# Seven block products for eight in the gate and up projections of a SwiGLU layer, with one weight tile's low part made by an adding DMA

## The chip, the core and the metric

The kernel runs on one core of a Trainium2 chip. The metric is the device time of the whole program in microseconds (us), the median of several runs. PE is TensorE, which multiplies matrices; PEld is its loading of the stationary operand; DVE is VectorE, ACT is ScalarE, POOL is GpSimd, and SP issues most DMAs. Every engine works through its own queue of instructions in the order in which they stand there, and waits on semaphores for the others.

## What is computed

One decoder layer over 256 tokens of width 2048, all in float32: a mixer (attention beside a convolution, then an output projection), and a SwiGLU block, which is where the change is. Cut to that block, the reference is

```
h  = rmsnorm(x, norm_pre_ffn)                       # 256 x 2048
g  = einsum('bsd,df->bsf', h, w_gate)               # 2048 x 5632
up = einsum('bsd,df->bsf', h, w_up)                 # 2048 x 5632
f  = einsum('bsf,fd->bsd', silu(g) * up, w_down)    # 5632 x 2048
x  = x + rmsnorm(f, norm_post_ffn)
```

## The kernel before

**Products.** A float32 number is split exactly in two: a high part (its float32r rounding) and a low part (the rest). A product of activations and weights is three matmuls per k tile of 128 rows: high by high, low by high, high by low. A weight tile is 512 rows (four k tiles) by 512 columns, 1 MB. Its high part `wh` is a rounding copy on ACT (L170), its low part `wl` is the difference on DVE (L171).

**Half steps.** The program is a row of half steps, each one weight tile against one of the two blocks of 128 tokens: 8 matmuls with `wh` (pass 0, L236 and L237), then 4 with `wl` (pass 1, L239). A weight tile serves two half steps. A chunk is 512 columns of gate or up, its sum over the 16 k tiles is four weight tiles, and its two token blocks have a PSUM bank each. After the gate and the up chunk with the same number f (11 of each), ACT takes silu of gate (L753), DVE multiplies by up (L761), PE transposes the product (L768) and it is split again (L193, L194). After every four chunks (then four, then three) the down projection of these rows runs, four chunks of 512 columns, added up in SBUF (L777, L779).

**What sets the order.** It is written out by the program `run_stream`, which goes through the half steps: first side work that is due, then the split of the weight tile that takes the slot just given up, then the loading of a further tile, then the 12 matmuls. `wh` and `wl` have four slots each (NSLOT), so a tile is split when the tile four places before it has had its last matmul. Loaded weights (`w`) have three buffers (NW), and a load is issued by SP when the split that read the buffer is done.

Of the kernel before, what the change touches and what calls it, by code (L numbers as in the profile page):

```python
# [26 lines left out]
P = 128  # L27
# [28 lines left out]
def hybrid_layer_kernel(ctx: ExitStack, tc: tile.TileContext, x, xt, pack, lamv,  # L56
# [28 lines left out]
    # ------------------------------------------------------------ constants  # L85
# [50 lines left out]
    class WTile:  # L136
        """Some rows (nk tiles of 128) and 512 columns of a weight matrix."""

        def __init__(self, src, r0, nk, cols):
            self.src, self.r0, self.nk, self.cols = src, r0, nk, cols  # L140
            self.eager = False

# [32 lines left out]
    class Operand:  # L175
        """8 k tiles per part of [128, 256 tokens], as float32r h and l."""
# [20 lines left out]
    class Chunk:  # L197
        """psum[tb] = x[tb] @ one 512-column chunk."""
# [16 lines left out]
    halves = []          # (chunk, tile, k of x, token block)  # L215
    tiles = []

    def add(chunk, specs, stagger=False):
        """specs: (k of x, WTile) in order."""
        for k, t in specs:  # L220
            tiles.append(t)
        order = ([(s, tb) for tb in range(2) for s in specs] if stagger
                 else [(s, tb) for s in specs for tb in range(2)])
        for (k, t), tb in order:
            halves.append((chunk, t, k, tb))
            chunk.left[tb] += t.nk

    def one(chunk, t, k0, tb, j, pas):
        """One k tile: pass 0 is (h + l) of x with h of w, pass 1 h of x with l of w."""
# [11 lines left out]
    def matmuls(chunk, t, k0, tb):  # L241
        if t.eager:
            # k tile by k tile, both token blocks, as the first data comes in
# [12 lines left out]

    def run_stream():
        last_use, preps = {}, deque()
# [3 lines left out]
        for s, (c, t, k, tb) in enumerate(halves):  # L262
            now[0] = s
            run_side()
            while preps:
# [3 lines left out]
                if i + NW < len(tiles):  # L269
                    tiles[i + NW].dma()  # L270
# [7 lines left out]
            if c.left[tb] == 0 and c.done:  # L278
                c.done(tb)
# [13 lines left out]
    # ------------------------------------------------------------ pre norm  # L293
# [27 lines left out]
    # ------------------------------------------------------------ lambda, bias  # L321
# [3 lines left out]
    def small_setup():  # L325
# [15 lines left out]
        # -(e0 - e1 + init) = (e1 - e0) - init  # L341
# [3 lines left out]
        # r[h, m] = bias of distance m - 127, masked below  # L345
# [8 lines left out]
        # bias[q, h, k] = r[h, 255 + q - k]  # L354
# [106 lines left out]
    # ------------------------------------------------------------ attention  # L461
# [34 lines left out]
    def head(h, qT, kT):  # L496
# [13 lines left out]
        for c in range(2):  # L510
            for b in range(2):
                # e = -(scores + bias), nm = min(e)
# [13 lines left out]
        # a * sum0 = e0 - (lam sum0 / sum1) e1; 1 / sum0 follows at the output  # L526
# [17 lines left out]
    def attend(half):  # L544
# [6 lines left out]
        # aT columns: [keys 0, block 1 | keys 1, block 1 | keys 0, block 0]  # L551
# [12 lines left out]
        # columns (head, block), block 0 the later queries  # L564
# [70 lines left out]
    # ------------------------------------------------------------ mixer output  # L635
# [42 lines left out]
    rstd2 = [None, None]  # L678

# [48 lines left out]

    oc = []
# [16 lines left out]
    # ------------------------------------------------------------ SwiGLU  # L746
# [38 lines left out]
    def post_down(pi, last, n, bank):  # L785
        for tb in range(2):
            down_evac(pi, last, n, tb, bank[tb])
        if pi == 1 and n == 0:
            load_gain(1, "gpf")
# [24 lines left out]
    parts = [(0, 4), (4, 8), (8, 11)]  # L814
    for pi, (f0, f1) in enumerate(parts):
        A = Operand("act")
        last = pi == len(parts) - 1
        needs = {}
        for f in range(f0, f1):
            c = both(lambda bank, f=f: post_gate(f, bank))(Chunk("gate", H2))  # L820
            add(c, w_tiles(w_gate, 0, [(f * C, C)], 0, KT), stagger=f == 0)
            k = (f - f0) * 4

            def hook(bank, f=f, A=A, k=k):
                g = post_up(f, A, k, bank)
                j = Job(g, now[0])
# [4 lines left out]
            add(c, w_tiles(w_up, 0, [(f * C, C)], 0, KT))  # L831
            needs[k] = [lambda f=f: st_["act", f]]
        nk = (f1 - f0) * 4
        for n in range(4):
            c = Chunk("down", A, needs=needs)
            ts = w_tiles(w_down, f0 * C, [(n * C, C)], 0, nk)
            if last and n == 3:
                c.done = lambda tb, c=c, pi=pi: spawn(finish(pi, tb, c.bank[tb]))
                add(c, ts, stagger=True)
            else:  # L840
                both(lambda bank, pi=pi, last=last, n=n: post_down(pi, last, n, bank))(c)
                add(c, ts)
# [10 lines left out]
    # the first tiles come in pieces, and are split k tile by k tile  # L853
# [71 lines left out]
```

## Time and profile before

| | us |
|---|---|
| median of 3 runs (lowest, highest) | 1088.16 (1087.69, 1088.36) |
| profiled execution, first to last instruction | 1086.7 |
| PE busy in it | 1072.2 |
| DVE busy in it | 634.9 |
| ACT busy in it | 491.6 |
| gate, up and down stage, about | 370 to 1078 |

The profile is of one execution. Its span lies about 1.5 us under the median of the runs; the rest lies before the first and after the last instruction. A busy PE here means that matmuls follow each other without a gap; matmuls overlap, so the distance between two starts is the cost of one, and not its duration.

### The profile page before, as it was taken

The page shows a single profiled execution, that of the slowest core. Times are in us where ns is not written, and L with a number is a line of the kernel's source. Part 1 is how long each engine was busy: PE and PEld are TensorE (multiplying, and loading weights), DVE is VectorE, ACT ScalarE, POOL GpSimd, SP SyncE. Part 2 cuts the span into 40 slices and gives each one's busy share as a digit, 9 for nine tenths or more (in the row PEclk, how much of TensorE's full clock was granted, in tenths as well). Part 3 has the DMA queues.
Part 4 walks back from the last instruction along what each step waited for, and adds up shares of the span by engine and source line. Part 5 has one row for each costly group of instructions (what it writes and reads, how often), then busy time and mean ns, then how long its engine had stood idle before and what let it go on. Part 6 is the DMA issues. An engine that isn't in the chain of part 4 may idle for free.

```text
span 1086.7 us, 11988 instructions
## 1 busy us (share of the span) xinstructions
PE 1072.2 (99%) x4886; PEld 885.5 (81%) x4886; DVE 634.9 (58%) x733; ACT 491.6 (45%) x525; POOL 10.8 (1%) x16
## 2 busy tenths in 40 slices
PE   9999999999999999999999999999999999999996
PEld 7878788787888888888888888888888888888885
DVE  6589989898556654444544445444454444454554
ACT  6754563755645743334334334343333333333441
POOL 0000000001000000000000000000000000000000
PEclk9999999999999999999999999999999999999998
DMA  9876545444764556555555555555656555555532
GB/s 307 300 259 210 180 161 183 157 156 156 296 203 155 173 198 209 183 195 175 186 193 192 195 194 191 194 183 178 215 179 232 195 194 191 177 194 194 194 116 77
DMA packets 113686, 209.77 MB, mean 193 GB/s; under 512 B 4024, under 2 KB 23776, under 8 KB 112864
## 3 DMA queue, kind: packets, MB, share of 16 engines
q1 hardware_dynamic: 113632, 209.02, 56.9%
q8 instruction: 38, 0.62, 0.2%
q14 instruction: 16, 0.13, 0.0%
HBM read 206.89 MB, written 2.11 MB: 192 GB/s over the span
## 4 chain that ended last, share of the span: by engine, by line
PE 90%; DMA 3%; DVE 3%; ACT 2%; issue 1%; SPq 1%; POOL 1%; DVEq 0%; POOLq 0%; ACTq 0%
PE mm L236 28%; PE mm L237 28%; PE mm L239 28%; DMA w<-in_w_in_dram 3%; DVE wl L171 1%; ACT wh L170 1%; PE ft L768 1%; DVE conv_acc L397 1%; DMA rb<-in_rel_bias_dram 1%; PE scmm L236 1%; PE scmm L237 1%; PE scmm L239 1%; PE sc L505 0%; POOL hrs L97 0%; PE ht L698 0%
## 5 line engine op out<-in xcount | busy, mean ns | idle before, releaser
L171 DVE TENSOR_TENSOR wl<-w,wh 128x2048 fp32r<-128x2048 f32 (+1 forms) x200 | 432.3, 2163 | 348.6 <-ACT wh L170 345.4
L170 ACT CAST wh<-w 128x2048 fp32r<-128x2048 f32 (+1 forms) x200 | 361.2, 1808 | 345.3 <-PE mm L237 322.5
L236 PE MATMUL mm<-wh,h2h 128*128 128x512 f32 x704 | 275.2, 391 | 0.0
L237 PE MATMUL mm<-wh,h2l 128*128 128x512 f32 x704 | 274.0, 389 | 0.0
L239 PE MATMUL mm<-wl,h2h 128*128 128x512 f32 x704 | 188.3, 389 | 0.0
L239 PEld LDWEIGHTS mm<-wl,h2h 128*128 128x128 f32 x704 | 132.2, 188 | 27.6
L237 PEld LDWEIGHTS mm<-wh,h2l 128*128 128x128 f32 x704 | 132.2, 188 | 27.1
L236 PEld LDWEIGHTS mm<-wh,h2h 128*128 128x128 f32 x704 | 132.2, 188 | 27.0
L236 PE MATMUL mm<-wh,acth 128*128 128x512 f32 x352 | 137.2, 390 | 0.0
L237 PE MATMUL mm<-wh,actl 128*128 128x512 f32 x352 | 137.0, 389 | 0.0
L236 PE MATMUL mm<-wh,xh 128*128 128x512 f32 x320 | 127.4, 398 | 1.4 <-ACT wh L170 1.4
L237 PE MATMUL mm<-wh,xl 128*128 128x512 f32 x320 | 124.9, 390 | 0.0
L397 DVE SCALAR_TENSOR_TENSOR conv_acc<-conv_in,pk,conv_acc 128x255 f32<-128x255 f32 (+14 forms) x240 | 94.2, 463 | 0.0
L239 PE MATMUL mm<-wl,acth 128*128 128x512 f32 x352 | 94.1, 389 | 0.0
L239 PE MATMUL mm<-wl,xh 128*128 128x512 f32 x320 | 87.2, 390 | 0.0
L239 PEld LDWEIGHTS mm<-wl,acth 128*128 128x128 f32 x352 | 66.1, 188 | 13.8
L237 PEld LDWEIGHTS mm<-wh,actl 128*128 128x128 f32 x352 | 66.1, 188 | 13.6
L236 PEld LDWEIGHTS mm<-wh,acth 128*128 128x128 f32 x352 | 66.1, 188 | 13.6
L236 PEld LDWEIGHTS mm<-wh,xh 128*128 128x128 f32 x320 | 60.1, 188 | 15.3 <-ACT wh L170 2.4
L239 PEld LDWEIGHTS mm<-wl,xh 128*128 128x128 f32 x320 | 59.9, 188 | 13.2 <-DVE wl L171 0.6
L237 PEld LDWEIGHTS mm<-wh,xl 128*128 128x128 f32 x320 | 60.2, 188 | 11.8
L237 PE MATMUL mm<-wh,mixl 128*128 128x512 f32 x96 | 37.5, 391 | 0.3 <-DVE mixl L458 0.3
(137 smaller groups left out, 556.6 us busy)
## 6 DMA issues: line engine op xcount, KB each, us to landing
w<-in_w_gate_dram SPq DMA_DIRECT2D x44, 1024.0 KB, 5.0
w<-in_w_up_dram SPq DMA_DIRECT2D x44, 1024.0 KB, 5.0
w<-in_w_down_dram SPq DMA_DIRECT2D x44, 1024.0 KB, 5.1
w<-in_w_in_dram SPq DMA_DIRECT2D x24, 1024.0 KB, 5.0
w<-in_w_out_dram SPq DMA_DIRECT2D x16, 1024.0 KB, 5.1
w<-in_w_in_dram SPq DMA_DIRECT2D x24, 512.0 KB, 4.8
w<-in_w_in_dram SPq DMA_DIRECT2D x16, 256.0 KB, 5.8
xn<-in_x_dram SPq DMA_DIRECT2D x2, 1024.0 KB, 11.2
```

Of the source, the lines that this page charges most:

```text
L170: nc.scalar.copy(self.h[:, a:b], self.w[:, a:b])
L171: nc.vector.tensor_tensor(out=self.l[:, a:b], in0=self.w[:, a:b], in1=self.h[:, a:b].bitcast(F32), op=ALU.subtract)
L236: nc.tensor.matmul(bank, lhsT=h, rhs=t.h[:, j], start=first, stop=False)
L237: nc.tensor.matmul(bank, lhsT=l, rhs=t.h[:, j], start=False, stop=False)
L239: nc.tensor.matmul(bank, lhsT=h, rhs=t.l[:, j], start=False, stop=last)
L397: return lambda: nc.vector.scalar_tensor_tensor(out=conv_acc[:, cb, s:], in0=conv_in[:, cb, :S - s], scalar=w, in1=conv_acc[:, cb, s:], op ...
L768: nc.tensor.transpose(bk[:, j * P:(j + 1) * P], sg[:, tb, j * P:(j + 1) * P], ident)
```

## The change

It alters the gate and up chunks f = 1 to 10; chunk 0 and all of down keep their products, and down runs after three, three, three and two chunks instead of four, four and three. The lower eight k tiles of a chunk pair are computed as before: two ordinary tiles of gate (called G0 and G1 here) and two of up (U0 and U1), two half steps each. The upper eight k tiles, for both chunks and both token blocks, are a product of a 2 by 2 matrix of activation blocks and a 2 by 2 matrix of weight tiles (r11 and r21 of gate, r12 and r22 of up), and instead of eight block products it is made from seven, in the program P1 to P7, of 12 matmuls each, from sums and differences of the blocks. The class `Pair` does that:

- Sums of the activations are made once (`form_sums`), and split.
- Sums of the weight tiles are made for every pair on DVE: three in a row (`sums`, after the split of the U0 before it) and one later (`last_sum`, after the split of P3). They overwrite loaded tiles, and one of them has a `w` buffer of its own that is not loaded (x).
- Each of the seven products has a high and a low part made from its tile or sum, and one half step.
- Results are put together outside PSUM: copies of partial sums on ACT (`v`, `s`), additions on DVE (L1011, L1028, L1037).
- The four half steps of U0 and U1 of one pair are placed among the products of the next pair (`fill`), so the order is P1, U0 (2), P7, P6, U1 (2), P5, P2, G0 (2), P3, G1 (2), P4: 15 half steps, where there were 16.
- G1's low part is not a DVE difference. ACT writes the negative of the rounded tile to `wl`, and a DMA issued by POOL adds the tile, read again from DRAM, to it.
- Loads go through two queues (`pump`): three `w` buffers, and a few whole tiles (`raw`) from the general pool, to which r12, r21 and r22 go.
- To have room, the residual is written to DRAM and read back near the end.

The diff, cut to this core:

```diff
         def split(self):
             self.h = wp.tile([P, SPLIT, C], F32R, tag="wh", bufs=NSLOT, name="wh")
             self.l = wp.tile([P, SPLIT, C], F32R, tag="wl", bufs=NSLOT, name="wl")
-            self.split_part(0, self.nk)
+            if self.by_dma:
...
+                nc.scalar.activation(self.l, self.w, ACTF.Copy, scale=-1.0)
+                nc.gpsimd.dma_start(self.l, rows[:, c0:c0 + n].rearrange("(k p) c -> p k c", p=P),
+                                    accum_op=ALU.add)
+                nc.scalar.copy(self.h, self.w)
+            else:
+                self.split_part(0, self.nk)
+            free["w"] += 1
...
+    def pump(i):
+
+        for tag, q in queue.items():
+            while q and free[tag] and q[0][0] - i <= 9:
+                free[tag] -= 1
+                q.popleft()[1].load(tag)
...
                 if i < len(tiles):
                     tiles[i].split()
-                if i + NW < len(tiles):
-                    tiles[i + NW].dma()
+                    pump(i)
+                    for fn in tiles[i].post:
+                        fn()
+                    pump(i)
...
+    def form_sums():
+
+        r = v3(T("sums"), 4)
+        h, l = H2.part(1)
...
+            nc.vector.tensor_tensor(out=r[:, o], in0=r[:, a], in1=r[:, b], op=op)
+        sh, sl = v3(T("sumh", F32R), 4), v3(T("suml", F32R), 4)
+        nc.scalar.copy(sh, r)
+        nc.vector.tensor_tensor(out=sl, in0=r, in1=sh.bitcast(F32), op=ALU.subtract)
...
+        def sums(self):
+            self.sub(self.r11, self.r12, self.r11)
+            self.sub(self.r12, self.r22, self.r12)
+            self.sub(self.x, self.r22, self.r11)
+
+        def last_sum(self):
+            self.sub(self.x, self.r21, self.x)
+            free["r"] += 1
...
+            return (s[1] + fill[0] + s[7] + s[6] + fill[1] + s[5] + s[2] + g[0] + s[3] + g[1] + s[4])
...
+            elif what == 7:
+                self.b7 = ps.tile([P, 2, C], F32, tag="sc", bufs=1, name="b7")[:, 0]
...
+            if what == 1:
+                self.v = v3(M("v"), 2)
+                nc.scalar.copy(self.v[:, 0], self.b1)
+            elif what == 6:
+                nc.scalar.copy(self.v[:, 1], self.b1)
+            elif what == 5:
+                self.s = M("s")[:, :C]
+                nc.scalar.copy(self.s, self.b1)
+                nc.vector.tensor_tensor(out=self.s, in0=self.b7, in1=self.s, op=ALU.add)
+            elif what == "g1" and tb == 0:
+                self.sg = v3(M("sg"), 2)
+                self.gate(0, self.b2, self.v[:, 0])
+            elif what == 4:
+                self.gate(1, self.b7, self.v[:, 1])
+            elif what == "u1" and tb == 0:
+                self.up(0, self.b1)
+            elif what == "u1":
+                nc.vector.tensor_tensor(out=self.s, in0=self.b8, in1=self.s, op=ALU.add)
+                self.up(1, self.s)
+                st_["act", self.f] = spawn(act_put(self.A, self.k, self.sg), 2)
...
+    parts = [(0, 3), (3, 6), (6, 9), (9, 11)]
```

What the engines have in their queues is shown at three places. On DVE before, inside the chunks f = 5, from one up chunk into the next gate chunk (`wl` is a low part, `sg` the gated product, `actl` the low part of its transpose; what a row waits for stands in brackets):

```order
L171 TENSOR_TENSOR wl_4809<-w_4704,wh_4808 128x2048 [waits DMAHW3_49,PE_49,Activation_49]
L171 TENSOR_TENSOR wl_4842<-w_4752,wh_4841 128x2048 [waits DMAHW4_49,PE_49,Activation_49]
L171 TENSOR_TENSOR wl_4874<-w_4782,wh_4873 128x2048 [waits DMAHW5_49,PE_49,Activation_49]
L171 TENSOR_TENSOR wl_4904<-w_4812,wh_4903 128x2048 [waits DMAHW6_49,PE_49,Activation_49]
L171 TENSOR_TENSOR wl_4934<-w_4845,wh_4933 128x2048 [waits DMAHW7_49,PE_49,Activation_49]
L761 SCALAR_TENSOR_TENSOR sg_4838<-mm0_4847,rffn0_2921,sg_4838 128x512 [waits PE_49]
L761 SCALAR_TENSOR_TENSOR sg_4838<-mm1_4848,rffn1_3047,sg_4838 128x512 [waits PE_49]
L171 TENSOR_TENSOR wl_4966<-w_4877,wh_4965 128x2048 [waits DMAHW0_49,Activation_49]
```

Now on DVE, from the U0 of pair f = 3, through the three sums of pair 4, to that pair's P5 (rows 1 and 8 are low parts of U0 and U1, rows 2 to 4 the sums, rows 5 and 7 the gate additions of pair 3, row 6 the low part of P7, the others those of P6 and P5):

```order
L196 TENSOR_TENSOR wl_4262<-w_4200,wh_4261 128x2048 [waits DMAHW4_49,PE_49,Activation_49]
L957 TENSOR_TENSOR w_4143<-raw_4175,w_4143 128x2048 [waits DMAHW2_49,DVE_49]
L957 TENSOR_TENSOR raw_4175<-raw_4178,raw_4175 128x2048 [waits DMAHW3_49,DVE_49]
L957 TENSOR_TENSOR w_4265<-raw_4178,w_4143 128x2048 [waits DMAHW0_49]
L1011 TENSOR_TENSOR sg_4281<-b2_4202,v_4071 128x512 [waits PE_49]
L926 TENSOR_TENSOR wl_4297<-raw_4175,wh_4296 128x2048 [waits DVE_49,DMASW2_49,PE_49,Activation_49]
L1011 TENSOR_TENSOR sg_4281<-b7_4109,v_4071 128x512 [waits PE_49]
L926 TENSOR_TENSOR wl_4317<-w_4265,wh_4316 128x2048 [waits DVE_49,Activation_49]
L196 TENSOR_TENSOR wl_4336<-w_4219,wh_4335 128x2048 [waits DMAHW5_49,PE_49,Activation_49]
L926 TENSOR_TENSOR wl_4367<-w_4143,wh_4366 128x2048 [waits PE_49,Activation_49]
```

The gate addition that reads the bank b7 stands behind U0's low part, three sums and P7's low part; the next pair's P7 writes that same bank, of which there is one.

On ACT before, around the end of one up chunk (`acth` is the high part of the transposed product):

```order
L170 CAST wh_4933<-w_4845 128x2048 [waits DMAHW7_49,DVE_49,PE_49]
L170 CAST wh_4965<-w_4877 128x2048 [waits DMAHW0_49,DVE_49,PE_49]
L193 CAST acth0_4737<-ft_4997 128x4x128 [waits PE_49]
L193 CAST acth0_4737<-ft_5004 128x4x128 [waits PE_49]
L170 CAST wh_5011<-w_4907 128x2048 [waits DMAHW1_49,DVE_49]
```

Now on ACT in pair 4: the copy of P5's partial sum, G1's negative, G1's high part, the transposed product, the high parts of P4 and of the next P1:

```order
L1027 COPY s_4456<-b1_4320 128x512 [waits DVE_49,PE_49]
L186 ACTIVATE wl_4460<-w_4370 128x2048 [waits DMAHW0_49]
L189 CAST wh_4459<-w_4370 128x2048 [waits Activation_49]
L218 CAST act_4484<-ft_4479 128x4x128 [waits PE_49]
L218 CAST act_4484<-ft_4487 128x4x128 [waits PE_49]
L925 CAST wh_4494<-w_4265 128x2048 [waits DVE_49,Activation_49]
L925 CAST wh_4524<-w_4406 128x2048 [waits DMAHW1_49,PE_49,Activation_49]
```

G1's `w` buffer is given up by the third of these rows, and that now follows a copy which waits for DVE.

On SP before, loads of gate and up, one after the other, each waiting for the DVE split that frees its buffer:

```order
L151 DMA w_4331<-in_w_gate_dram 128x4x512 [waits DMAHW4_49,DVE_49]
L151 DMA w_4363<-in_w_gate_dram 128x4x512 [waits DMAHW5_49,DVE_49]
L151 DMA w_4393<-in_w_up_dram 128x4x512 [waits DMAHW6_49,DVE_49]
L151 DMA w_4423<-in_w_up_dram 128x4x512 [waits DMAHW7_49,DVE_49]
L151 DMA w_4455<-in_w_up_dram 128x4x512 [waits DMAHW0_49,DVE_49]
```

Now on SP: G0 and G1 of pair 3, then r11, r12 and r22 of pair 4, then U0 and U1 of pair 3:

```order
L166 DMA w_4077<-in_w_gate_dram 128x4x512 [waits DMAHW7_49,DMAHW5_49,DVE_49]
L166 DMA w_4107<-in_w_gate_dram 128x4x512 [waits DVE_49]
L166 DMA w_4143<-in_w_gate_dram 128x4x512 [waits DMAHW7_49,DVE_49]
L166 DMA raw_4175<-in_w_up_dram 128x4x512
L166 DMA raw_4178<-in_w_up_dram 128x4x512 [waits DMAHW3_49,PE_49]
L166 DMA w_4200<-in_w_up_dram 128x4x512 [waits DMAHW4_49,DMAHW0_49,Activation_49]
L166 DMA w_4219<-in_w_up_dram 128x4x512 [waits DVE_49]
```

U0's load (the row before the last) stands behind three loads that are issued together, and waits for ACT, which is G1's high part.

## Rows read from the trace of the kernel before

**Rows 1.** The page: span, then engine, busy us (share of the span), instructions.

```profile
span 1086.7 us, 11988 instructions
...
PE 1072.2 (99%) x4886; PEld 885.5 (81%) x4886; DVE 634.9 (58%) x733; ACT 491.6 (45%) x525; POOL 10.8 (1%) x16
```

**Rows 2.** Stretches: length, busy PE, PEld, DVE, ACT, POOL; clock, DMA share, GB/s.

```profile
272.00:274.00 2.00, 2.00 (x11) 1.64 (x10) 1.50 (x3) 2.00 (x3) 0.00 (x0) 1.00 1.04 402
...
400.00:1060.00 660.00, 660.00 (x2953) 547.18 (x2952) 314.03 (x179) 258.94 (x177) 0.00 (x0) 1.00 0.56 189
...
1076.00:1087.00 11.00, 1.99 (x9) 1.31 (x7) 4.34 (x7) 0.72 (x2) 0.54 (x1) 0.71 0.31 119
```

**Rows 3.** The chain that ended last, 486 to 494 us: start, us, what.

```profile
486.67 0.92 PE mm L239 x4
487.58 0.87 PE ft L768 x8
...
490.30 0.92 PE mm L239 x4
...
493.03 0.91 PE mm L239 x4
```

**Rows 4.** Groups by line and shape, 400 to 1060: busy us, mean ns; idle before.

```profile
L171 DVE TENSOR_TENSOR wl<-w,wh 128x2048 fp32r<-128x2048 f32 x120 | 275.1, 2292 | 290.5 <-ACT wh L170 290.5
...
L170 ACT CAST wh<-w 128x2048 fp32r<-128x2048 f32 x120 | 229.5, 1912 | 287.9 <-PE mm L237 285.3 <-issue 2.6
...
L761 DVE SCALAR_TENSOR_TENSOR sg<-mm,rffn,sg 128x512 f32<-128x512 f32 x20 | 15.0, 748 | 14.5 <-PE mm L239 14.5
L194 DVE TENSOR_TENSOR actl<-ft,acth 128x512 fp32r<-128x512 f32 x22 | 14.2, 686 | 34.9 <-ACT acth L193 34.9
L753 ACT ACTIVATE sg<-mm,rffn 128x512 f32<-128x512 f32 x20 | 13.8, 690 | 37.4 <-PE mm L239 37.4
L193 ACT CAST acth<-ft 128x512 fp32r<-128x512 f32 x21 | 11.3, 590 | 48.8 <-PE ft L768 48.8
```

**Rows 5.** Who waited for whom, 400 to 1060: us in total, times, longest.

```profile
DVE wl L171 <- ACT wh L170: 290.5, 120, 4.6
ACT wh L170 <- PE mm L237: 285.3, 91, 3.5
...
SPq L151 <- DVE wl L171: 593.2, 117, 7.3
```

**Rows 6.** DMA issues of the whole run: count, KB each, median us to landing.

```profile
w<-in_w_gate_dram SPq DMA_DIRECT2D x44, 1024.0 KB, 5.0
...
xres<-in_x_dram SPq DMA_DIRECT2D x2, 1024.0 KB, 10.3
...
gpost<-in_gains_dram SPq DMA_DIRECT2D x1, 1024.0 KB, 7.3
```

**Rows 7.** DVE in order of time, 330 to 405: start, us, what, idle before.

```profile
369.06 4.48 DVE L171 TENSOR_TENSOR wl<-w,wh 128x2048 fp32r<-128x2048 f32 x2
375.07 2.29 DVE L171 TENSOR_TENSOR wl<-w,wh 128x2048 fp32r<-128x2048 f32 x1 [1.53 <-ACT wh L170]
...
393.35 0.75 DVE L761 SCALAR_TENSOR_TENSOR sg<-mm,rffn,sg 128x512 f32<-128x512 f32 x1 [1.52 <-PE mm L239]
```

**Rows 8.** DVE in order of time, the last 30 us: start, us, what, idle before.

```profile
1069.87 0.69 DVE L799 TENSOR_TENSOR fsum<-mm,fsum 128x512 f32<-128x512 f32 x1 [5.67 <-PE mm L239]
...
1078.03 0.69 DVE L799 TENSOR_TENSOR fsum<-mm,fsum 128x512 f32<-128x512 f32 x1 [2.75 <-PE mm L239]
```

More of the change, by code (lines that the diff above doesn't have):

```diff
@@ L141, in __init__, with load @@
             self.eager = False
+            self.by_dma = False
+            self.loads = [("w", self)]
+            self.post = []
+        def load(self, tag):
+            if tag == "w":
+                self.dma()
+            else:
+                self.w = v3(T("raw"), SPLIT)
+                self.dma_part(0, self.nk)
         def dma(self):
@@ L216, in hybrid_layer_kernel, with put, steps_of @@
     tiles = []
-    def add(chunk, specs, stagger=False):
-        for k, t in specs:
-            tiles.append(t)
+    def put(steps):
+        for c, t, k, tb in steps:
+            if t not in tiles:
+                tiles.append(t)
+            halves.append((c, t, k, tb))
+    def steps_of(chunk, specs, stagger=False):
         order = ([(s, tb) for tb in range(2) for s in specs] if stagger
@@ L224, in add @@
         for (k, t), tb in order:
-            halves.append((chunk, t, k, tb))
             chunk.left[tb] += t.nk
+        return [(chunk, t, k, tb) for (k, t), tb in order]
+    def add(chunk, specs, stagger=False):
+        put(steps_of(chunk, specs, stagger))
     def one(chunk, t, k0, tb, j, pas):
@@ L241, in matmuls @@
     def matmuls(chunk, t, k0, tb):
+        if isinstance(chunk, Pair):
+            chunk.matmuls(t, k0, tb)
+            return
         if t.eager:
@@ L255, in matmuls @@
         chunk.left[tb] -= t.nk
+    free = {"w": 0, "r": 2}
+    queue = {"w": deque(), "r": deque()}
+    def pump(i):
[3 more added lines that the diff above has]
+                q.popleft()[1].load(tag)
     def run_stream():
+        for i, t in enumerate(tiles):
+            if i >= NSLOT + NW:
+                for tag, raw in t.loads:
+                    queue[tag].append((i, raw))
         last_use, preps = {}, deque()
@@ L277, in run_stream @@
             now[0] = s + 1
-            if c.left[tb] == 0 and c.done:
+            if isinstance(c, Pair):
+                c.after(k, tb)
+            elif c.left[tb] == 0 and c.done:
                 c.done(tb)
@@ L727, in residual @@
         rstd2[tb] = partial_rstd(part2, tb, "rffn")
+        nc.sync.dma_start(xd[tb], xr)
+        st_["x", tb] = None
+        if tb:
+            yield 2
+            form_sums()
     oc = []
@@ L812, in finish, with __init__, at, load @@
         yield 1
-    parts = [(0, 4), (4, 8), (8, 11)]
+    class Act:
+        def __init__(self):
+            self.t = {}
+        def at(self, k, n, tok):
+            f = k // 4
+            if f not in self.t:
+                self.t[f] = T("act", F32R).rearrange("p (s k t) -> p s k t", s=2, k=4)
+            t = self.t[f]
+            return t[:, 0, k % 4:k % 4 + n, tok], t[:, 1, k % 4:k % 4 + n, tok]
+        put_psum = Operand.put_psum
+    class Slot:
+        def load(self, tag):
+            self.w = wp.tile([P, SPLIT, C], F32, tag="w", bufs=NW, name="w")
@@ new lines, in hybrid_layer_kernel, with __init__, split @@
+    class Product:
+        nk, eager = SPLIT, False
+        def __init__(self, pair, n, src, tag=None, loads=()):
+            self.pair, self.n, self.src, self.tag = pair, n, src, tag
+            self.loads, self.post = list(loads), []
+        def split(self):
+            w = self.src.w
+            self.h = wp.tile([P, SPLIT, C], F32R, tag="wh", bufs=NSLOT, name="wh")
+            self.l = wp.tile([P, SPLIT, C], F32R, tag="wl", bufs=NSLOT, name="wl")
+            nc.scalar.copy(self.h, w)
+            nc.vector.tensor_tensor(out=self.l, in0=w, in1=self.h.bitcast(F32), op=ALU.subtract)
+            if self.tag:
+                free[self.tag] += 1
@@ new lines, in act_put, with reload @@
+    def act_put(A, k, sg):
+        for tb in range(2):
+            bk = aux_bank("ft")
+            for j in range(4):
+                nc.tensor.transpose(bk[:, j * P:(j + 1) * P], sg[:, tb, j * P:(j + 1) * P], ident)
+            A.put_psum(k, 4, slice(tb * P, (tb + 1) * P), v3(bk, 4))
+        yield 1
+    def reload():
+        load_gain(1, "gpf")
+        for tb in range(2):
+            st_["x", tb] = T("xres")
+            nc.sync.dma_start(st_["x", tb], xd[tb])
+    parts = [(0, 3), (3, 6), (6, 9), (9, 11)]
@@ L819, in hybrid_layer_kernel @@
         for f in range(f0, f1):
+            k = (f - f0) * 4
+            needs[k] = [lambda f=f: st_["act", f]]
+            if f:
+                pair = Pair(f, A, k)
+                put(pair.steps(fill))
+                fill = pair.up_steps()
+                continue
             c = both(lambda bank, f=f: post_gate(f, bank))(Chunk("gate", H2))
-            add(c, w_tiles(w_gate, 0, [(f * C, C)], 0, KT), stagger=f == 0)
-            k = (f - f0) * 4
+            add(c, w_tiles(w_gate, 0, [(f * C, C)], 0, KT), stagger=True)
             def hook(bank, f=f, A=A, k=k):
-                g = post_up(f, A, k, bank)
-                j = Job(g, now[0])
+                j = Job(post_up(f, A, k, bank), now[0])
                 st_["act", f] = j
@@ L836, in hybrid_layer_kernel @@
             ts = w_tiles(w_down, f0 * C, [(n * C, C)], 0, nk)
+            if last and n == 0:
+                ts[0][1].post.append(reload)
             if last and n == 3:
@@ L839, in hybrid_layer_kernel @@
                 add(c, ts, stagger=True)
-            else:
-                both(lambda bank, pi=pi, last=last, n=n: post_down(pi, last, n, bank))(c)
-                add(c, ts)
+                continue
+            both(lambda bank, pi=pi, last=last, n=n: post_down(pi, last, n, bank))(c)
+            st = steps_of(c, ts)
+            if n == 3:
+                put(st[:-4])
+                fill = [st[-4:-2], st[-2:]]
+            else:
+                put(st)
     zero = M("zero")
```

87 lines of the change are left out of this document (82 added, 5 removed).

## The prediction, made before the changed kernel ran

> **What bounds the kernel now.** I read the page first: PE is busy 99% of the span [rows 1]. An average can hide a stage with another limit, so next the stretch of 400 to 1060, which lies wholly in the stage that is changed: PE is busy all of its 660 us at a granted clock of 1.00, DVE 314, ACT 259, and the DMA engines 0.56 [rows 2]. The chain that ended last shows what PE does there: half steps and transposes with no gap [rows 3]. Pass 1 of a half step, four matmuls, takes 0.91 us, so a matmul is 0.227, a half step of twelve 2.72, and eight transposes 0.91 (their two rows, 0.87 and 0.91, hardly differ).
>
> The waits say that PE leads: ACT's casts wait for PE 285 us, DVE's low parts for ACT 290 us, SP's loads for DVE 593 us [rows 5]. Nothing there costs time as long as PE is last. So what counts is whether PE stays last with a sixteenth less work and more for all others.
>
> **What goes.** Ten pairs lose one half step each: 10 x 2.72 = 27.2 us, all of it on the path. A pair falls from 16 x 2.72 + 0.91 = 44.4 us to 41.7.
>
> **What comes, as busy time.** DVE has 14 operations of 2048 columns in a pair (ten low parts, four sums) and eight small ones. A low part is 2.29 [rows 4]; two back to back take 4.48 [rows 7], so 2.2 when queued. The sums have the same operands but a plain output; no row shows one. A cast over the same size takes 1.91 and a low part 2.29 [rows 4]; I take 2.2, as they are the same operation. The small ones are 0.69 and 0.75 [rows 4], 0.6 to 0.7 queued. That makes 14 x 2.2 + 8 x 0.65 = 36 of 41.7 us. ACT: 12 x 1.9 and eight small ones of 0.59 or 0.69 [rows 4], about 28. Loads: 8 MB and an addition; in the stretch of 272 to 274 the loads moved 402 GB/s with the queue full [rows 2], which is 2.6 us for 1 MB, so 21 us of 41.7. No engine is full. But DVE's 5.6 us are spread thin, and the order is fixed, so I follow the chains of one pair.
>
> **The chains of one pair.** T is the start of P7, which needs bank b7, read last by the gate addition of the pair before. A load alone lands after 5.0 us [rows 6].
>
> (i) Behind T on ACT: silu 0.7, P6's cast 1.9; then DVE: P6's low part 2.3, U1's 2.2. This frees the buffer into which G0 is loaded: 5.0, cast 1.9, low part 2.3. DVE then does three evacuations, of which the product with up releases the transposes: 2.2. Together 18.4. PE has six half steps until there, 16.3. The transposes are 2.0 late. P6 is 0.3 late as well, behind the copy of P1's sum that stands after its cast.
>
> (ii) P3's low part 2.2, the last sum 2.2, the addition to s 0.7: 5.1, on DVE after those evacuations. The addition reads b7, into which G0's second half step writes. PE has the transposes and one half step, 3.6. That is 1.4 late.
>
> (iii) From the start of that half step (T0) to the next P7, PE has eight half steps, 21.8. DVE and ACT must do two low parts of the transposed product, P4's and the next P1's, U0's (not before T0 + 9.0), three sums 6.6, the gate addition 0.7, silu 0.7, P7's cast and low part 4.2, the second gate addition 0.7: together 21.9. This is balanced, provided U0 has landed at T0 + 4.7.
>
> (iv) Whether it has. U0 takes G1's buffer, given up by G1's high part. On ACT that stands behind the copy of P5's sum, which waits for DVE's last product with up (T0 - 5.1); 0.6, the negative 1.9, the high part 1.9 bring T0 - 0.7. On SP the load stands behind r11, r12 and r22, issued together at T0 - 7.3 when G0's low part ends; they land at T0 - 2.3, + 0.3 and + 2.9 by 2.6 each, so U0 follows at T0 + 5.5. It is 0.8 late, **plus whatever the adding DMA takes of the engines** (call it a), since it is issued at T0 - 2.6 and stands ahead of U0's data.
>
> **The adding DMA.** No row shows one. From below: nothing, if it moves beside the loads (engines 0.56 busy [rows 2]). Its data in is that of one load, 2.6. If reading the destination counts as much as reading the source, it is two loads, 5.2. From above: xres, 1 MB behind another, landed after 10.3 [rows 6]; a lone load's 5.0 holds 2.4 that is not engine time, which leaves 7.9, three loads. I take **a = 3.9**, between one load and two, since it reads twice and writes once where a load does each once. G1's own low part is due at T0 + 7.25, so it holds PE itself only if a passes about 4.
>
> A rule bears on this. The Trainium skill's page "DMA: Bandwidth & Descriptors", under "Issuing engines are not separate DMA queues", says that DMAs of the gpsimd engine run on the same 16 engines as the others and interleave with them; no row here shows a second queue at work. By it POOL's queue gives no way past, and a isn't nothing. The same page, under "Anatomy of one DMA — SWDGE (gpsimd) path", fits 2.0 us plus bytes / 436e3; an estimate from it, for a plain 1 MB, is a = 2.4, and the sum below would be 1103.
>
> **The sum.** Ten pairs:
> - Six have a pair before them in their part (f = 2, 4, 5, 7, 8, 10). Each loses 0.3 + 2.0 + 1.4 = 3.7 by (i) and (ii).
> - Two of them, the third of their part (f = 5, 8), lose 0.8 + a = 4.7 by (iv): 8.4 each.
> - The four others follow a pair that was not late, whose DVE was about 2.1 earlier, so U0 costs a - 1.3 = 2.6: 6.3 each.
> - The first pairs of parts two to four (f = 3, 6, 9) come out of down, with buffers filled ahead: nothing.
> - f = 1 comes out of an ordinary chunk, with the sums of the activations in DVE's queue (2 x 1.15 + 4 x 0.6 and 2.2, with a cast of 1.9 between), behind U0 and ahead of or beside three sums. Before, DVE is nearly packed at that place [rows 7]. P7 comes 4.4 to 7 late; I take 6, and 3.4 for its own (i) and (ii).
>
> Stalls: 4 x 6.3 + 2 x 8.4 + 9.4 = 51.4. Against the profiled span of 1086.7: 1086.7 - 27.2 + 51.4 = 1110.9. That span lies 1.5 us under the median, so the time is **1112**, slower. The residual's detour through DRAM costs nothing: DVE's work near the end, the addition at 1069.9 and what follows it, fits ahead of the last one at 1078.0 [rows 8], and the reload is issued four down chunks earlier. Its cover is those chunks; without it, it is one load, 10.3 [rows 6]. Down after three chunks instead of four adds 4 x 2 small DVE additions off the path.
>
> **Rivals.**
> 1. *The adding DMA is hidden* (a = 0). For: the engines are 0.56 busy. Against: at that spot three loads are queued. Then the stalls are 4 x 3.7 + 2 x 4.5 + 9.4 = 33.2, **1094**.
> 2. *The slack absorbs the chains*, the other side. The place is chains (i) to (iii), which I price by the durations of single instructions. If DVE passes its 2048 columns in 1.9, as ACT does [rows 4], and a load lands in 4.0 when the engines are idle, (i) is 1.0 + 3 x 0.35 = 2.1 shorter and no longer late, (ii) 0.6 shorter, and (iii) has 2 us of room, which takes up (iv) without a. For: DVE has 5.6 us of room in a pair, PE never waited long before, and SP waited up to 7.3 for DVE [rows 5], so loads had slack. Against: 2.2 is measured, back to back. The price: 1.1 in each of six pairs and 6 to 9.4 at f = 1, **1075**; wholly absorbed but for f = 1's 6, 1067. It decides where the six pairs lose (27.2 - 9.4) / 6 = 3.0 on average; I reckon 7.0.
> 3. *G1's low part is itself late* (a of 7.8): it holds PE in seven pairs, about 4 us each: **1139** or more.
> 4. *The clock*. In 1076 to 1087, where PE was busy 1.99 of 11 us, the granted clock was 0.71 [rows 2], so PE that pauses can fall towards 1.2 of 2.4 GHz. A half step at half clock costs 2.7 more. One after each of the longest waits (f = 1, 2, 4, 5, 7, 8, 10) is 19 us: 1131. I count it as the upper part of the forecast.
>
> That the half step does not go away is no rival: it is in the order, fifteen for sixteen.
>
> **How the numbers follow.** Forecast (a from 2.6 to 5.2, with the clock's case): 0.55, 1104 to 1131. Hidden: 0.15, around 1094, with 0.05 of it inside 0.2%, which is about what a measurement of this kernel can tell from no change (2.2 us). Absorbed, in part or whole: 0.22, 1067 to 1086. G1 late: 0.08, 1139 and more. Faster: 0.22 and 0.02 of the hidden case, 0.24. Same: 0.05. Slower: 0.71. The range leaves out some 0.12 below, half of the absorbed case, and 0.08 above: 1076 to 1139. As cases of slower hold most, the likeliest's own range is 1104 to 1131.
>
> **What would show it.** In the profile after: PE waits of 1 to 5 us, on gate additions (P7), on the transposes behind the product with up, and on G0's second half step behind the addition to s; SP's U0 loads landing 8 us or more after their issue; DVE near 36 us a pair with few gaps in the second and third pairs, and many in the first. Half steps stay at 2.72. Right in size only: the waits there, but 1 us each. Wrong: PE without gaps between 400 and 1060 and a pair in 41.7 us (absorbed), or the longest waits at G1's second pass (the addition).

## The result, and the profile after

The changed kernel takes 1139.05 us (1138.83 to 1139.63), the kernel before beside it 1088.26: the ratio is 1.0465, with a 95% interval of 1.045 to 1.048. It is slower, as forecast, but by 50.8 us where I had forecast 24, and 0.05 us above the upper end of the range.

The page of the kernel after: span, and the busy time of each engine.

```profile
span 1137.3 us, 12035 instructions
...
PE 1070.6 (94%) x4766; PEld 869.0 (76%) x4766; DVE 801.0 (70%) x848; ACT 579.0 (51%) x596; POOL 23.8 (2%) x26
```

Against [rows 1], PE has 120 matmuls less and is busy 1.6 us less, not 27: behind its waits it runs slower, which counts as busy (24 us in the table below). The busy share fell from 99% to 94%, so PE no longer bounds the stage. The place of its waits is read from the list of who waited for whom, PE alone, 375 to 1070 us (engine, instruction, what it waited for: us in total, times, longest):

```profile
PE b L1004 <- DMA wl<-in_w_gate_dram: 19.2, 8, 4.5
PE b L1004 <- DVE s L1028: 9.2, 6, 1.5
PE ft L1045 <- DVE sg L1016: 8.7, 12, 1.6
PE b L1004 <- ACT sumh L750: 6.8, 1, 6.8
PE b L1004 <- DVE sg L1011: 5.9, 4, 2.8
PE b L1007 <- DVE suml L751: 1.5, 1, 1.5
```

Each line is one place of the prediction: G1's pass 1 behind the adding DMA; G0's second half step behind the addition to s (chain ii); the transposes behind the product with up (i); the entry at f = 1 (two lines); P7 behind the gate addition (iii, iv). In [rows 5] no wait of PE stands at all.

Idle time is not the whole loss, since what follows a wait runs slower for a while. So I also added up, place by place, by how much two starts of matmuls lie further apart than 0.227 us (0.114 for a transpose):

| place | idle, us | loss with what follows, us | predicted, us |
|---|---|---|---|
| entry, P7 of f = 1 | 8.3 | 11.0 | 6 |
| G1's low part, ten pairs | 19.2 | 33.5 | 0 |
| transposes (i), six pairs | 8.7 | 11.4 | about 12 |
| G0's second half step (ii), six pairs | 9.2 | 10.9 | about 8 |
| P7 (iii, iv), six pairs | 5.9 | 8.6 | 19.8 |
| sum | 51.3 | 75.4 | 51, with 3.4 of f = 1's own and 1.8 at P6 |

75.4 less the 27.2 of the half steps is 48.2, and 50.8 was measured; the rest is in pieces of under 1 us, one at the first down chunk of the last part.

**One pair, closely.** Pair f = 4 has the longest wait. First POOL, ACT, PE and SP in order of time, 618 to 660 us (start, length, instruction, in brackets the idle time before):

```profile
629.91 1.28 POOL L187 DMA_DIRECT2D wl<-in_w_gate_dram  x1 [49.85 <-ACT wl L186]
```

```profile
627.21 0.59 ACT L1027 COPY s<-b 128x512 f32<-128x512 f32 x1 [2.64 <-DVE sg L1016]
627.69 1.93 ACT L186 ACTIVATE wl<-w 128x2048 fp32r<-128x2048 f32 x1
629.51 1.89 ACT L189 CAST wh<-w 128x2048 fp32r<-128x2048 f32 x1
...
644.55 1.90 ACT L195 CAST wh<-w 128x2048 fp32r<-128x2048 f32 x1 [8.27 <-DMA w<-in_w_up_dram]
656.15 0.72 ACT L1012 ACTIVATE sg<-sg,rffn 128x512 f32<-128x512 f32 x1 [9.69 <-DVE sg L1011]
```

```profile
632.17 0.50 PE L1004 MATMUL b<-wh,h2h 128*128 128x512 f32 x1 [1.55 <-DVE s L1028]
...
639.34 0.39 PE L1007 MATMUL b<-wh,h2l 128*128 128x512 f32 x1
644.25 2.07 PE L1004 MATMUL b<-wl,h2h 128*128 128x512 f32 x4 [4.52 <-DMA wl<-in_w_gate_dram]
646.12 0.63 PE L1004 MATMUL b<-wh,h2h 128*128 128x512 f32 x1
```

```profile
625.52 1.05 SPq L166 DMA_DIRECT2D raw<-in_w_up_dram  x2
631.42 5.47 SPq L166 DMA_DIRECT2D w<-in_w_up_dram  x2
636.94 0.53 SPq L166 DMA_DIRECT2D raw<-in_w_gate_dram  x1
```

T0 of the prediction is 632.2 (G0's second half step). The copy of P5's sum waits for DVE and the negative follows, as reckoned in (iv). The adding DMA is issued at T0 - 2.3 (reckoned: - 2.6), U0's load at T0 - 0.8 (- 0.7), PE needs G1's low part at T0 + 7.4 (+ 7.25). All this came as worked out. What did not: the addition lands at T0 + 12, 4.5 late, and U0, issued after it, no sooner (ACT's cast of it starts at 644.55). DVE stands idle for that cast, and the sums that the next P7 needs stand behind its row:

```profile
646.49 2.29 DVE L196 TENSOR_TENSOR wl<-w,wh 128x2048 fp32r<-128x2048 f32 x1 [7.79 <-ACT wh L195]
```

Why it takes so long is seen in the DMA view of 632 to 644 alone (busy tenths and GB/s in 40 slices of 0.3 us; then the queues: packets, MB, share of 16 engines' time; q0 is POOL's, q1 that of SP):

```profile
DMA  9999999999999999999999999999999999999999
GB/s 396 369 403 362 410 369 375 355 403 259 212 273 246 280 239 239 253 246 259 266 246 273 266 259 266 246 266 266 266 266 239 273 259 273 259 335 389 396 396 410
...
q1 hardware_dynamic: 1291, 2.55, 60.1%
q0 software_dynamic: 528, 1.05, 47.3%
```

The 16 engines are busy throughout. Up to 634.7 the loads run alone at about 390 GB/s, as in [rows 2]; then, until 642.5, loads and addition together move about 260. The addition of 1 MB takes 47.3% of 12 us, 5.7 us of all engines; a load, 60.1% of 12 us for 2.55 MB, 2.8 per MB. The two queues by themselves, first from 630 to 634, just behind the addition's issue, then from 637 to 642:

```profile
q1 hardware_dynamic: 777, 1.56, 104.9%
```

```profile
q0 software_dynamic: 318, 0.65, 70.0%
q1 hardware_dynamic: 319, 0.65, 39.7%
```

At first the addition moves nothing, while the loads issued before it move on; then it and the loads move the same bytes, 0.65 MB each in 5 us. So it does not stand ahead of U0's data, as I had put it: both run through each other until both are nearly done. The Trainium skill says so, on its page "DMA: Bandwidth & Descriptors", under "Issuing engines are not separate DMA queues" (they interleave with each other); the trace agrees, and I had quoted it and still reckoned with a queue. Over the whole run the addition's issue to landing:

```profile
L187 POOL DMA_DIRECT2D wl<-in_w_gate_dram x10: 1282/1282/1465, 418.5 to 1055.8; - x10
...
DMA to landing us min/median/max: 9.8/12.2/14.3
```

Issued at T0 - 2.3 and due at T0 + 7.4, it has 9.7 us. Its shortest time is 9.8. So it is late in every pair, the first of a part too, for which I had priced nothing. How late goes by the loads ahead of it: in the last pair of each part (f = 2, 5, 8, 10), where no pair follows whose r11, r12 and r22 are loaded by then, it landed 9.8 to 10.1 us after its issue and cost 0.3 to 0.7 us; in the six others it landed after 11.9 to 14.3 and cost 2.9 to 7.4.

**The clock.** Stretches behind the longest waits (length, busy PE, PEld, DVE, ACT, POOL; granted clock, DMA share, GB/s):

```profile
432.00:438.70 6.70, 6.56 (x16) 5.15 (x17) 4.17 (x2) 1.90 (x1) 0.00 (x0) 0.53 0.81 306
...
644.00:650.00 6.00, 5.75 (x14) 4.50 (x15) 3.51 (x2) 1.90 (x1) 0.00 (x0) 0.50 0.74 280
```

After a wait of 4.5 us PE runs at 1.2 GHz: the starts lie 0.43 us apart instead of 0.23. In the table the loss less the idle time is 24 us, of which about 15 stand at the six places where the clock fell. Whether that is a price of its own is asked below (e3).

### The profile page after: what moved, and what is told of

Its sections match the earlier page's. It is cut to its first block, busy times and chain, and to the rows that moved or that the text cites. A ratio compares the mean times of both kernels' runs of the same rounds, so it can differ in the third digit from the quotient of the medians.

```text
span 1137.3 us, 12035 instructions
## 1 busy us (share of the span) xinstructions
PE 1070.6 (94%) x4766; PEld 869.0 (76%) x4766; DVE 801.0 (70%) x848; ACT 579.0 (51%) x596; POOL 23.8 (2%) x26
## 5 line engine op out<-in xcount | busy, mean ns | idle before, releaser
L196 DVE TENSOR_TENSOR wl<-w,wh 128x2048 fp32r<-128x2048 f32 (+1 forms) x150 | 317.2, 2119 | 212.2 <-ACT wh L195 212.2
L195 ACT CAST wh<-w 128x2048 fp32r<-128x2048 f32 (+1 forms) x150 | 265.0, 1772 | 193.5 <-PE mm L270 80.6
L1004 PE MATMUL b<-wh,h2h 128*128 128x512 f32 x440 | 177.3, 403 | 9.2 <-DVE s L1028 9.2
L1007 PE MATMUL b<-wh,h2l 128*128 128x512 f32 x440 | 176.0, 400 | 0.0
L1004 PE MATMUL b<-wl,h2h 128*128 128x512 f32 x440 | 123.0, 402 | 19.4 <-DMA wl<-in_w_gate_dram 19.2
L269 PE MATMUL mm<-wh,act 128*128 128x512 f32 x352 | 137.4, 390 | 0.2 <-ACT act L218 0.2
L270 PE MATMUL mm<-wh,act 128*128 128x512 f32 x352 | 137.1, 389 | 0.2 <-DVE act L219 0.2
L926 DVE TENSOR_TENSOR wl<-w,wh 128x2048 fp32r<-128x2048 f32 x40 | 91.4, 2289 | 45.7 <-ACT wh L925 45.7
L1004 PEld LDWEIGHTS b<-wh,h2h 128*128 128x128 f32 x440 | 85.0, 193 | 30.3 <-DVE s L1028 11.7
L1007 PEld LDWEIGHTS b<-wh,h2l 128*128 128x128 f32 x440 | 85.2, 194 | 17.9
L272 PE MATMUL mm<-wl,act 128*128 128x512 f32 x352 | 94.1, 389 | 0.0
L270 PEld LDWEIGHTS mm<-wh,act 128*128 128x128 f32 x352 | 66.1, 188 | 14.1 <-DVE act L219 0.5
L269 PEld LDWEIGHTS mm<-wh,act 128*128 128x128 f32 x352 | 66.1, 188 | 14.0 <-ACT act L218 0.5
## 6 DMA issues: line engine op xcount, KB each, us to landing
raw<-in_w_gate_dram SPq DMA_DIRECT2D x10, 1024.0 KB, 11.9
```

The costliest lines, as they stand in the source:

```text
L195: nc.scalar.copy(self.h[:, a:b], self.w[:, a:b])
L196: nc.vector.tensor_tensor(out=self.l[:, a:b], in0=self.w[:, a:b], in1=self.h[:, a:b].bitcast(F32), op=ALU.subtract)
L269: nc.tensor.matmul(bank, lhsT=h, rhs=t.h[:, j], start=first, stop=False)
L270: nc.tensor.matmul(bank, lhsT=l, rhs=t.h[:, j], start=False, stop=False)
L272: nc.tensor.matmul(bank, lhsT=h, rhs=t.l[:, j], start=False, stop=last)
L926: nc.vector.tensor_tensor(out=self.l, in0=w, in1=self.h.bitcast(F32), op=ALU.subtract)
```

## The experiments

Each was timed beside the kernel before (1088.5 to 1088.6 us). Where nothing else is said, an edit is made to the changed kernel. This table gives PE's idle time by place, from the list shown above for the kernel after, in each kernel's own trace:

| kernel | time, us | entry | G1's low part | P7 | G0's second | transposes | last down |
|---|---|---|---|---|---|---|---|
| after | 1139.1 | 8.3 | 19.2 | 5.9 | 9.2 | 8.7 | 0.4 |
| e1_dve | 1108.9 | 8.1 | - | 9.5 | 9.2 | 4.0 | 0.4 |
| e2_plain | 1121.4 | 8.1 | 3.2 | 19.7 | 7.2 | 1.1 | 0.4 |
| e3_busy | 1137.8 | 8.3 | 3.0 | 18.3 | 9.5 | 2.2 | 0.4 |
| e4_later | 1119.6 | 0 | 15.6 | 12.6 | 7.6 | 3.1 | 0.4 |
| e5_silu | 1079.2 | 8.3 | - | 0 | 3.4 | 0.6 | 0.4 |
| e6_i_ii | 1113.0 | 8.1 | - | 15.4 | 3.8 | 0 | 8.9 |
| e7_all | 1083.3 | 8.2 | - | 1.3 | 0 | 0 | 5.1 |
| e8_all_later | 1074.1 | 0 | - | 1.7 | 0 | 0 | 5.7 |
| e9_silu_add | 1106.8 | 8.2 | 17.3 | 0 | 1.0 | 0 | 0.4 |
| e10_best | 1069.7 | 0 | - | 0 | 2.9 | 0 | 0.4 |
| e11_sum | 1065.1 | 0 | - | 0 | 0 | 0 | 0.4 |

### e1_dve: G1's low part on DVE again

```diff
-            self.g[1].by_dma = True
+            self.g[1].by_dma = False
```

> The changed kernel, with G1's low part as a DVE difference again (ten more DVE passes of 2048, ten negatives on ACT and ten adding DMAs fewer); nothing else. Theory A (the adding DMA lands too late, 12.2 us after its issue, and holds PE itself at G1's pass 1): the 33 us that PE loses there go, most of the 9 us at P7 go too since the loads are free of it, and DVE's 2.2 more in the chain to P7 bring some 13 back: 1110. Theory B (DVE's and ACT's chains are the bound, and the wait at G1 only shows what would be lost a few steps later): 1130 to 1145.

Measured: 1108.9 us, ratio 1.0189 (1.0172 to 1.0206). Theory A's 1110 holds: 30 us of the 51 are the adding DMA's, and ten DVE passes cost less than it did. Still 20 us slower than before, with the four other waits in place.

### e2_plain: a plain copy on the same queue

```diff
-                nc.gpsimd.dma_start(self.l, rows[...], accum_op=ALU.add)
+                nc.gpsimd.dma_start(self.l, rows[...])
```

> The changed kernel, with the POOL DMA of G1 copying the tile instead of adding it (same queue, same bytes from DRAM, same place and waits; the low part of G1 is therefore left out and replaced by the tile). Theory A1 (it is the adding, which reads its destination, that takes long: about two loads' engine time): the DMA lands in 7 to 9 us instead of 12.2, the wait at G1 mostly goes: 1105 to 1118. Theory A2 (it is the queue and what stands ahead in the engines, or POOL's issue): landing 11 to 13 us, 1135 to 1140.

Measured: 1121.4 us (ratio 1.0300, 1.0284 to 1.0315). The line on POOL's DMA in it:

```profile
DMA to landing us min/median/max: 5.7/9.1/11.7
```

The queues over 400 to 1100 us, in this kernel and then in the one after:

```profile
q1 hardware_dynamic: 63792, 128.98, 52.4%
q0 software_dynamic: 5280, 10.49, 4.9%
```

```profile
q1 hardware_dynamic: 63606, 128.63, 52.3%
q0 software_dynamic: 5280, 10.49, 8.4%
```

The same ten DMAs take 4.9% of 700 us as copies, 3.4 us each, and 8.4% as additions, 5.9. The adding itself so costs 2.5 us of the engines and 3.1 us to the landing: A1, not A2. The wait at G1 nearly goes, 19.2 to 3.2. But the time fell by 18 and not by the 21 to 34 that I gave it, since P7 now waits 19.7 where it waited 5.9: one wait had hidden the other. The page "DMA: Bandwidth & Descriptors" of the Trainium skill, under "Anatomy of one DMA — SWDGE (gpsimd) path", has 2.0 us plus bytes / 436e3, 4.4 us for this copy as an estimate; the shortest here was 5.7, 1.3 above it, in a pair without loads ahead of it; the addition, 9.8 at best, took more than twice as long.

### e3_busy: PE kept working in its waits

```diff
+                if pas == 1 and what == "g1" and tb == 0:
+                    fill({1: 12, 3: 8, 4: 18, 6: 10, 7: 14, 9: 13}.get(self.f, 0))
```

> The changed kernel, with 8 to 18 matmuls that compute nothing used (into a spare bank) put ahead of G1's pass 1 in the six pairs where PE waited 2 us or more for the adding DMA (f = 1, 3, 4, 6, 7, 9), so that PE works through its wait. The wait's length stays. Theory C (PE that pauses there is granted 1.2 GHz for several us behind it, which costs 13 us in the stage in addition to the idle time): the granted clock stays 1.00 behind these waits, 1127 to 1131. Rival (the slow stretches have another cause): 1139 or more, with the clock at 0.5 as before.

Measured: 1137.8 us, 1.3 us less, where theory C wanted 8 to 12. The mechanism is right: in pair 4, PE works through its wait (18 matmuls in a row), and the half steps behind it are at full speed. The stretch of 640 to 662 us:

```profile
640.00:662.00 22.00, 19.79 (x87) 15.82 (x85) 11.59 (x6) 4.43 (x3) 0.00 (x0) 1.00 0.46 147
```

But PE then comes to P7 sooner and stands there, in PE's order of time:

```profile
663.04 0.47 PE L1012 MATMUL b<-wh,sumh 128*128 128x512 f32 x1 [3.24 <-DVE sg L1019]
```

P7's waits rose from 5.9 to 18.3 us, and slow stretches appeared behind four of these. So the slow clock behind G1 was worth 1.3 us by itself: what set P7 was U0's late load and the chain behind it, which doesn't care how fast PE got there. What the slow stretches behind P7 cost was not tested.

### e4_later: the first pair ordinary

```diff
-            if f:
+            if f > 1:
                 pair = Pair(f, A, k)
...
+            if fill:
+                put(fill[0] + fill[1])
```

> The changed kernel, with f = 1 an ordinary pair of 16 half steps too, so that the sums of the activations have a chunk pair's time before the first P7 (f = 2). Theory A: the 11 us at the first P7 and the 6 us of f = 1's adding DMA go, f = 2 now loses what a first pair loses, 3 us, instead of 5; a half step more costs 2.7: 1122 to 1127. Rival (the entry's wait only moves to f = 2, since sums of weights and activations meet there as well): 1134 to 1140.

Measured: 1119.6 us (1.0286, 1.0270 to 1.0301), 2.4 below the range given. The entry does not move to f = 2.

### e5_silu: the silu behind the casts, with G1 on DVE

```diff
         def gate(self, tb, bank, part):
             nc.vector.tensor_tensor(out=self.sg[:, tb], in0=bank, in1=part, op=ALU.add)
+            spawn(self.silu(tb), 2)
+
+        def silu(self, tb):
             nc.scalar.activation(self.sg[:, tb], self.sg[:, tb], ACTF.Silu,
                                  scale=rstd2[tb][:, 0:1])
+            yield 1
```

> The run with G1's low part on DVE (e1_dve), with one move more: the two silu of a pair stand two half steps later in ACT's queue, behind the casts of the next P7 and P6, so that these casts don't wait for DVE's gate additions. Theory D (the ring of gate addition, silu, cast, low part, each waiting for the other engine, makes P7 late; DVE idles 2.6 us twice in it): the 17 us that PE loses at P7 in e1_dve go, some of it comes back at the transposes: 1092 to 1098. Rival F (DVE, 38 of 41.7 us in a pair, is full, and what is mended here is lost at another wait): 1105 to 1110.

Measured: 1079.2 us, ratio 0.9913 (0.9898 to 0.9927). Faster than before, and 29.7 us better than e1_dve: nearly twice what theory D gave, and rival F falls. DVE in order of time in e1_dve, at the P7 of f = 5:

```profile
640.31 0.68 DVE L1011 TENSOR_TENSOR sg<-b,v 128x512 f32<-128x512 f32 x1
643.58 2.29 DVE L926 TENSOR_TENSOR wl<-raw,wh 128x2048 fp32r<-128x2048 f32 x1 [2.60 <-ACT wh L925]
645.79 0.68 DVE L1011 TENSOR_TENSOR sg<-b,v 128x512 f32<-128x512 f32 x1
649.05 2.29 DVE L926 TENSOR_TENSOR wl<-w,wh 128x2048 fp32r<-128x2048 f32 x1 [2.58 <-ACT wh L925]
```

and in e5_silu:

```profile
631.70 0.68 DVE L1011 TENSOR_TENSOR sg<-b,v 128x512 f32<-128x512 f32 x1
632.30 2.28 DVE L926 TENSOR_TENSOR wl<-raw,wh 128x2048 fp32r<-128x2048 f32 x1
634.50 0.68 DVE L1011 TENSOR_TENSOR sg<-b,v 128x512 f32<-128x512 f32 x1
635.10 2.28 DVE L926 TENSOR_TENSOR wl<-w,wh 128x2048 fp32r<-128x2048 f32 x1
```

Before the move, the gate addition on DVE releases a silu on ACT, behind which stands the cast that DVE's next low part needs: from the first addition to P6's low part 8.7 us. Without that 3.4. The move takes 2.6 us out of chain (iii) and 2.6 out of (i), and with it PE's waits at P7 and nearly all at the transposes go. DVE holds: from one pair's sums to the next, 581.66 to 624.97, it is busy 38.5 of 43.3 us.

### e6_i_ii, e7_all, e8_all_later: the other two chains

e6 makes these two edits to e1_dve, e7 the same two to e5_silu, and e8 is e7 with the edit of e4:

```diff
-            p[3].post = [self.last_sum]
+            self.g[1].post = [self.last_sum]
...
-                st_["act", self.f] = spawn(act_put(self.A, self.k, self.sg), 2)
+                st_["act", self.f] = spawn(act_put(self.A, self.k, self.sg), 3)
```

> e1_dve with chains (i) and (ii) mended instead: the last sum stands behind G1's split, and so behind the addition to s that releases bank b7; the transposes of the product stand one half step later. Theory D: the 11 us at G0's second half step and the 7 us at the transposes go, but PE then reaches P7 some 3 us sooner in each of six pairs, and the ring there is what it was: 1100 to 1106. Rival G (the waits add up, each by itself): 1091.

> e1_dve with both: silu later, the last sum behind the addition to s, the transposes a half step later. Theory D: only the 11.6 us at the first P7 (f = 1) and a few us are left: 1075 to 1080. Rival F (DVE is full): 1088 or more.

> e7_all with f = 1 an ordinary pair: nine pairs of fifteen half steps. Theory D: the entry costs 2.7 for its half step and at most 2 for waits: 1066 to 1071. Rival F: 1080 or more.

Measured: 1113.0, 1083.3 and 1074.1 us, each slower than expected (the traced run of e8 took 1076.55, the longest of its four). e6 falls on neither side: it is 4 us slower than e1_dve. The waits at the two mended places shrink from 13.2 to 3.8, but P7's rise from 9.5 to 15.4 (the ring there is what it was, as theory D said), and a new one opens, which I hadn't counted. Who PE waited for, in e6:

```profile
PE b L1004 <- DVE sg L1011: 15.4, 6, 5.2
PE mm L269 <- ACT act L218: 7.3, 1, 7.3
...
PE mm L270 <- DVE act L219: 1.6, 1, 1.6
```

The last two are the first down chunk of the last part, which has only two chunk pairs, and waits for the transposes that were moved. e7 and e8 have the same wait (5.1 and 5.7).

### e9_silu_add: only the silu moved, the adding DMA kept

The edit is that of e5_silu alone.

> The changed kernel as it is, adding DMA included, with the silu two half steps later in ACT's queue and nothing else. In the kernel with G1's low part on DVE the same move gave 29.7 us (1108.9 to 1079.2). Theory H (the adding DMA's time from issue to landing, about 12 us, is too long by itself, whatever the rest does): PE still waits at G1's pass 1 in most pairs, some 30 us with the slower clock behind it: 1105 to 1120. Rival J (the addition is only late because the late ring queues its loads ahead of it): 1075 to 1085, no wait over 1 us at G1.

Measured: 1106.8 us (1.0166, 1.0151 to 1.0181): theory H. The issue to landing is unchanged, and PE's wait for it nearly so, though every other wait inside the pairs is gone but for 1.0 us:

```profile
DMA to landing us min/median/max: 9.8/12.1/14.3
```

```profile
PE b L1004 <- DMA wl<-in_w_gate_dram: 17.3, 7, 4.5
PE b L1004 <- ACT sumh L750: 6.7, 1, 6.7
PE b L1007 <- DVE suml L751: 1.5, 1, 1.5
PE b L1004 <- DVE s L1032: 1.0, 2, 0.7
```

With the rest in order, the addition costs 27.6 us against DVE (e5_silu).

### e10_best, e11_sum, e12_early: a kernel faster than both

e10 is e5_silu with the edit of e4; e11 is e10 with the last sum moved (the first of the two edits above, without the second); e12 is e5_silu with `form_sums` called right behind the last transposes of the activations.

> e5_silu (low part on DVE, silu later) with f = 1 an ordinary pair. If the waits are independent where PE leads: 1079.2 less the entry's 10.8, plus a half step of 2.7 : 1070 to 1072. Rival (the entry moves to f = 2): 1076 to 1080.

> e10_best with the last sum behind the addition to s, as in e6_i_ii, but the transposes where they were. If it is the later transposes alone that cost 7 us or more at the first down chunk of the last part in e6 to e8: the same as e10_best within 2 us, without a wait at G0's second half step or at that down chunk. If it is the later last sum: a wait of 5 us or more stays at the last part, 1074 to 1078.

> e5_silu with the sums of the activations formed as soon as the last block of activations is split, ahead of the squares for the norm, instead of behind P7's low part: they then stand ahead of P1's and U0's low parts and of the three sums of weights on DVE, and not behind them. DVE has 21 us of work ahead of P7's low part either way and 19 us for it: the entry's 10.8 us fall to 2 to 6: 1070 to 1075. Rival (the sums' split delays P1 and U0 by as much): 1079 or more.

Measured: 1069.7 (0.9823), 1065.1 (0.9784, 0.9767 to 0.9800) and 1076.2 us (0.9886). e10 is a little better than expected. e11 settles the question of e6 to e8, that it was the transposes, and gains 4.6 us where I had expected no more than 2. e12 came 1.2 us above its range: the entry's loss falls from 10.8 us to 5.6, of which 4.5 now lie at P1, and f = 1 gets a wait of 1.5 at G0's second half step; an ordinary pair is the better entry. e11_sum is the fastest kernel here, 2.2% under the one before. Its page, its stretch from 400 to 1010 us, and all of PE's waits up to 1070:

```profile
PE 1049.1 (99%) x4778; PEld 865.2 (81%) x4778; DVE 805.1 (76%) x847; ACT 555.3 (52%) x580; POOL 10.8 (1%) x16
```

```profile
400.00:1010.00 610.00, 610.00 (x2726) 505.18 (x2725) 459.01 (x270) 308.99 (x217) 0.00 (x0) 1.00 0.57 197
```

```profile
PE mm L269 <- ACT act L218: 0.2, 1, 0.2
PE mm L270 <- DVE act L219: 0.2, 1, 0.2
```

As in [rows 2], PE is busy all of the stretch at a clock of 1.00, now with DVE at 75% instead of 48%. Nine half steps of 2.72 are 24.5 us, and 23.5 were gained.

## Why the prediction was wrong

The sign was right, the size half of what came. By its steps:

- **What goes, 27.2 us**: right. In e11_sum nine half steps gave 23.5 of 24.5.
- **Busy times of DVE, ACT**: right. A sum takes 2.28 us, as a low part does. From the P7 of f = 4 to that of f = 5 DVE is busy 36.5 us (36) and ACT 25.9 (about 28), and e5_silu and e11_sum show that it is enough.
- **Chains (i) and (ii)**: right in place, and nearly in size: 1.6 to 2.9 a pair (2.0) and 1.8 (1.4).
- **Entry**: right in place, too small: 11.0 for 6, some 2.7 of it the slower clock.
- **The adding DMA**: the step that failed. "I take **a = 3.9**, between one load and two" measured 5.7 to 5.9, more than two loads, and above the 5.2 that my own forecast reached to. And "stands ahead of U0's data" took the engines for a queue, so that the addition would be done before U0; they interleave, and its landing was 12.2 us after its issue (median). The second weighs more: with 5.9 in that queue, behind r22 at T0 + 2.9, it would have landed at T0 + 8.8 by my own terms, 1.5 late; in pair 4 it was 4.5 late. "G1's own low part ... holds PE itself only if a passes about 4" had the right due time and thus put a condition that was fulfilled; I gave it, as rival 3, a chance of 0.08 and its time as 1139 or more. That 1139 came is luck in part: rival 3 had a = 7.8, seven pairs of 4 us and all of (iv) on top; measured were 5.9, ten pairs of 0.3 to 7.4, and 8.6 at P7.
- **First pairs "nothing"**: wrong by the same step. f = 3, 6 and 9 lost 3.9, 2.9 and 6.1 us, all of it at G1.
- **(iv), 19.8 us at P7**: right as a chain (in pair 4 from ACT's cast of U0 to P7, at 661.74, 17.2 us; reckoned from U0's landing, 21.8 - 4.7 = 17.1), but hidden in the run: PE was held at G1 before. e2 and e3, which take the wait at G1 away, show 19.7 and 18.3 us there. My sum added waits that stand in one ring, of which a run shows the longest.
- **The clock, 19 us at most**: it fell to its lower level at the entry and behind five of the waits at G1 (1.99 to 4.5 us; not behind one of 2.6), as said, but e3, which kept it up behind G1, gained 1.3 only, since the wait at P7 grew by what PE had saved.
- **Rival 2 (absorbed)**: as a time it was wrong, but e5_silu to e11_sum show what it would have taken: 5.3 us out of the ring by the order of one ACT instruction, with G1's low part back on DVE (with the addition kept, e9, it was still 1106.8), where I had sought shorter loads and DVE passes. I had priced the silu at 0.7 us in two chains; that it forces ACT's next cast to wait for DVE stood in my own list of chain (i), and I didn't ask what it would give to take it out.

What stays open: why an addition takes 5.9 us of the engines where a copy by the same queue takes 3.4 and a load 2.8; no run here took it apart. Nor was it tried to start the addition sooner with another buffer for the low part.

## What to carry to other kernels

A DMA that takes work off a busy engine is to be priced by its time from issue to landing amid the loads that it will meet, against the time at which its result is due, and not by its bytes. In a ring over several engines the waits don't add up: taking one away shows the next, so ask what the ring is without it, and look first for instructions of one engine that wait for another ahead of work that the other needs. Where two engines work by turns, the order in one queue (here a 0.7 us silu ahead of a cast) can be worth more than the whole change.

## What had not been expected of the hardware

- An adding DMA of 1 MB from DRAM into SBUF took 5.9 us of all 16 DMA engines, a copy on the same queue 3.4. Beside it, loads and addition together moved about 260 GB/s, half of it each, where the loads alone moved 390.
- The adding DMA landed 9.8 to 14.3 us after its issue; the copy 5.7 to 11.7.
- DVE, busy 75% of the stretch from 400 to 1010 us in e11_sum, did not hold PE up once: PE had no gap there and a granted clock of 1.00.
